# One step of a hybrid DeltaNet and attention block on one core: the opening in groups of 4, 2 and 2, two direct tiles per FFN, and a pinned order at the delta rule

## The chip, the core and the metric

The kernel runs on one core of a Trainium2 chip. TensorE (PE in the rows) multiplies matrices, VectorE (DVE) and ScalarE (ACT) work elementwise, GpSimd (POOL) also, and the queue of SyncE (SP) issues nearly all DMAs. The metric is the device time of one execution in microseconds: the median of three runs was 1587.57 (1587.5 to 1593.31).

## The reference, cut to what matters

One layer works on 128 prompt tokens and 512 latent tokens, 640 in all, of width 1024. Every sublayer begins with an RMS norm whose result is scaled and shifted by vectors that come from a conditioning vector through a large matrix (`ada_w`, nine vectors of 1024 for each of two conditionings).

```python
mod = silu(c) @ ada_w + ada_b             # shift, scale, gate, three times
x = x + 0.5*gate1 * swiglu(modulate(rms_norm(x, norm_ffn1), shift1, scale1), w13, w2)
h = modulate(rms_norm(x, norm_mix), shift2, scale2)
...
x = x + gate2 * merged
x = x + 0.5*gate3 * swiglu(modulate(rms_norm(x, norm_ffn2), shift3, scale3), w13, w2)

def swiglu(h, w13, w2):                   # w13: 1024 x 5632, w2: 2816 x 1024
    a, b = split(h @ w13, 2)
    return (silu(a) * b) @ w2
```

The delta rule is a gated linear attention over chunks, run forwards and backwards for four heads. In each chunk the lower triangular matrix `eye + strict(beta * (k k^T) * decay)` is inverted; the state then passes from chunk to chunk.

## The kernel before, in words

All activations lie transposed: the 1024 channels are eight blocks of 128 partitions, the 640 tokens are two halves of 320 columns. Precision comes from splitting: each operand is a high part (`hh`, `wh`) and a low part (`hl`, `wl`), and each product is three matmuls, high by high, low by high and high by low (`accumulate_step`, line 176). ScalarE makes the high part by a cast, VectorE the low part by a subtraction (`parts`, lines 127 and 131).

**The opening** (lines 1437 to 1460 and `modulation_part`). The inputs are loaded, transposed by TensorE and squared by ScalarE for the norm. The shift and scale vectors of the first FFN are made in four groups of two channel blocks: eight DMAs bring 2 MB of `ada_w`, TensorE multiplies (line 321), VectorE copies the result (line 329), TensorE transposes it (line 332), VectorE adds the bias and forms the scale (lines 337 to 345). Then `modulated` writes the operands of these two blocks: VectorE multiplies (line 403), ScalarE adds the shift and rounds (line 407), VectorE takes the low part (line 409). The first FFN weights are split by ScalarE and GpSimd. The matmuls of the first product are held behind the modulation's by `kpins`.

**An FFN** (`ffn`). The hidden width of 2816 is 22 tiles of 128. The first `DIRECT` tiles take the two products of a tile one after the other over eight blocks. The others (`product_pair`, line 206) take both at once as 2x2 block products by a scheme of seven products over four blocks each; GpSimd prepares four combined weights (lines 570 to 573). The scheme needs combined operands: T1 to T3 (`combined_operands`, lines 529 to 538, behind the second tile) and T4 (`last_operand`, lines 551 to 557, behind the last direct tile). Each tile ends with its low part `gl` (line 495). The tiles go in rounds (`ROUNDS`): after each, `w2` takes the round's tiles to the eight output blocks, and VectorE adds the result to the residual (line 444). The first FFN also carries the other modulation matmuls between its tiles (`between`, line 280). In the last round the last four output blocks go by halves, so that the norm of the next sublayer can begin on one half.

**The delta rule** (`delta`). `delta_front` builds the decay matrices E (subtraction of a column per head at line 986) and the triangular matrix, masked by GpSimd (line 1009); `delta_prep` inverts it in seven levels, each with matmuls, a masking by VectorE that writes P (line 1048), and copies by ScalarE; `delta_step` moves the states, with three products by GpSimd (lines 1090 to 1102). A few remaining z projections run between the first front and the first level; the gate products are spread between the delta rule's matmuls.

**What sets the order.** A planner orders the instructions of each engine when the kernel is built: of those that are ready in its plan, the one earliest in the program goes first. `high_priority(offset=n)` moves instructions n places forward; `issue_after(ins)` puts the instructions of a block behind `ins` on their engine. On the chip every engine works in that fixed order, and an instruction that waits holds all behind it. Tiles with a tag share a number of buffers, and a new tile waits until an old one is released.

## Time and profile before

| | us |
|---|---|
| median of three runs | 1587.57 |
| the profiled execution | 1587.36 |
| its span | 1585.6 |
| TensorE busy | 1541.3 |
| VectorE busy | 1093.8 |
| ScalarE busy | 655.0 |
| GpSimd busy | 290.9 |

The span runs from the first to the last instruction of the profiled execution; busy times are sums over an engine's instructions. A line number in a row is that of the kernel before. An entry such as `wl<-wraw,wh` names what is written and what is read. The time in brackets is how long the engine stood idle before, with what ended that.

### The profile page before, as it was taken

The page shows a single profiled execution, that of the slowest core. Times are in us where ns is not written, and L with a number is a line of the kernel's source. Part 1 is how long each engine was busy: PE and PEld are TensorE (multiplying, and loading weights), DVE is VectorE, ACT ScalarE, POOL GpSimd, SP SyncE. Part 2 cuts the span into 40 slices and gives each one's busy share as a digit, 9 for nine tenths or more (in the row PEclk, how much of TensorE's full clock was granted, in tenths as well). Part 3 has the DMA queues.
Part 4 walks back from the last instruction along what each step waited for, and adds up shares of the span by engine and source line. Part 5 has one row for each costly group of instructions (what it writes and reads, how often), then busy time and mean ns, then how long its engine had stood idle before and what let it go on. Part 6 is the DMA issues. An engine that isn't in the chain of part 4 may idle for free.

```text
span 1585.6 us, 28490 instructions
## 1 busy us (share of the span) xinstructions
PE 1541.3 (97%) x11242; PEld 1460.2 (92%) x11242; DVE 1093.8 (69%) x2317; ACT 655.0 (41%) x1210; POOL 290.9 (18%) x242
## 2 busy tenths in 40 slices
PE   6999999999999899999899999999999999999998
PEld 4889999999998898789889999899899999999997
DVE  6967675757667658886666655775697776767666
ACT  5434242323334545655445544323353433334335
POOL 2022222213120110000221222100005131323210
PEclk9999999999999899999999999999999999999999
DMA  9655444544225341114433324445022323232312
GB/s 328 192 163 174 127 151 147 166 148 133 95 83 148 90 120 48 55 54 130 152 119 99 99 79 122 144 146 160 27 72 76 110 60 111 61 100 67 94 54 67
DMA packets 220784, 181.17 MB, mean 114 GB/s; under 512 B 16160, under 2 KB 198109, under 8 KB 220651
## 3 DMA queue, kind: packets, MB, share of 16 engines
q1 hardware_dynamic: 220395, 179.29, 36.7%
q8 instruction: 89, 1.46, 0.4%
q14 instruction: 44, 0.36, 0.1%
q0 software_dynamic: 256, 0.06, 0.0%
HBM read 161.59 MB, written 16.42 MB: 112 GB/s over the span
## 4 chain that ended last, share of the span: by engine, by line
PE 88%; DVE 7%; DMA 2%; ACT 1%; issue 1%; POOL 0%; SPq 0%; DVEq 0%; POOLq 0%; ACTq 0%
PE big L176 32%; PE aux L206 21%; PE aux L176 12%; PE aux L163 9%; PE big L206 8%; PE aux L280 2%; DVE ht L403 1%; DVE hl L409 1%; PE aux L160 1%; DVE wl L131 1%; DVE cacc L860 1%; DMA wraw<-ffn_w 1%; DMA araw<-ada_w 1%; PE aux L1337 0%; DMA qe<-grows 0%
## 5 line engine op out<-in xcount | busy, mean ns | idle before, releaser
L127 ACT CAST wh<-wraw 128x1024 fp32r<-128x1024 f32 (+1 forms) x147 | 151.8, 1033 | 282.4 <-PE aux L176 99.0
L131 DVE TENSOR_TENSOR wl<-wraw,wh 128x1024 fp32r<-128x1024 f32 (+1 forms) x145 | 180.0, 1242 | 79.8 <-ACT wh L127 78.4
L176 PE MATMUL big<-hh,wh 128*128 128x320 f32 x768 | 191.0, 322 | 7.1 <-ACT hh L407 3.5
L176 PE MATMUL big<-hl,wh 128*128 128x320 f32 x768 | 194.5, 322 | 2.0 <-DVE hl L409 1.4
L176 PE MATMUL big<-hh,wl 128*128 128x320 f32 x768 | 189.0, 317 | 0.4 <-DVE wl L131 0.4
L570 POOL TENSOR_TENSOR ss<-wraw 128x512 f32<-128x512 f32 x38 | 51.0, 1342 | 713.2 <-DMA wraw<-ffn_w 522.5
L127 ACT CAST sh<-ss 128x512 fp32r<-128x512 f32 x152 | 92.6, 621 | 181.0 <-POOL ss L571 85.6
L131 DVE TENSOR_TENSOR sl<-ss,sh 128x512 fp32r<-128x512 f32 x152 | 132.0, 878 | 47.6 <-ACT sh L127 46.7
L206 PE MATMUL aux<-th,sh 128*128 128x320 f32 x456 | 140.9, 309 | 2.0 <-DVE x L444 2.0
L176 PEld LDWEIGHTS big<-hh,wh 128*128 128x128 f32 x768 | 130.3, 192 | 13.4 <-ACT hh L407 6.5
L206 PE MATMUL aux<-tl,sh 128*128 128x320 f32 x456 | 140.9, 309 | 0.0
L206 PE MATMUL aux<-th,sl 128*128 128x320 f32 x456 | 140.7, 309 | 0.0
L176 PEld LDWEIGHTS big<-hl,wh 128*128 128x128 f32 x768 | 132.3, 191 | 7.1 <-DVE hl L409 4.7
L176 PEld LDWEIGHTS big<-hh,wl 128*128 128x128 f32 x768 | 132.3, 191 | 5.3 <-issue 4.2
L176 PE MATMUL big<-gh,wh 128*128 128x320 f32 x352 | 89.0, 313 | 0.0
L444 DVE SCALAR_TENSOR_TENSOR x<-big,gate,x 128x128 f32<-128x128 f32 (+2 forms) x181 | 67.7, 424 | 30.0 <-PE big L176 29.7
L176 PE MATMUL big<-gl,wh 128*128 128x320 f32 x352 | 87.7, 310 | 0.0
L206 PEld LDWEIGHTS aux<-th,sh 128*128 128x128 f32 x456 | 85.6, 188 | 2.3 <-DVE x L444 2.3
L176 PE MATMUL big<-gh,wl 128*128 128x320 f32 x352 | 87.4, 309 | 0.0
L206 PEld LDWEIGHTS aux<-tl,sh 128*128 128x128 f32 x456 | 85.6, 188 | 0.0
L206 PEld LDWEIGHTS aux<-th,sl 128*128 128x128 f32 x456 | 85.6, 188 | 0.0
L1048 DVE TENSOR_TENSOR P<-aux,lv 128x512 f16<-128x512 f32 x70 | 48.2, 689 | 50.1 <-PE aux L163 50.1
(374 smaller groups left out, 3918.6 us busy)
## 6 DMA issues: line engine op xcount, KB each, us to landing
wraw<-ffn_w SPq DMA_DIRECT2D x120, 512.0 KB, 3.9
araw<-ada_w SPq DMA_DIRECT2D x56, 512.0 KB, 5.6
wraw<-w_in SPq DMA_DIRECT2D x35, 512.0 KB, 3.8
araw<-ada_w SPq DMA_DIRECT2D x32, 256.0 KB, 6.5
gd<-stage SPq DMA_DIRECT2D x16, 320.0 KB, 2.8
wraw<-ffn_w SPq DMA_DIRECT2D x12, 384.0 KB, 3.2
wraw<-w_out SPq DMA_DIRECT2D x8, 512.0 KB, 4.3
xd<-x SPq DMA_DIRECT2D x8, 320.0 KB, 2.3
```

Of the source, the lines that this page charges most:

```text
L127: nc.scalar.copy(hi, raw)
L131: nc.vector.tensor_sub(lo, raw, hi.bitcast(F32))
L160: self.marks.append(self.nc.tensor.transpose(*args))
L163: self.marks.append(self.nc.tensor.matmul(*args, **kw))
L176: self.nc.tensor.matmul(ps[h], lhsT=wt[:, k, c0 : c0 + P], rhs=xt[:, h, :], start=(k == 0 and j == 0), stop=(k == len(xs) - 1 and j == 2),)
L206: nc.tensor.matmul(ps, lhsT=wt[:, k * P : (k + 1) * P], rhs=xt, start=(k == 0 and j == 0), stop=(k == n - 1 and j == 2),)
L280: nc.tensor.matmul(ps[32 * g : 32 * g + 32], lhsT=self.s32[:, k, :], rhs=raw[:, g * 256 : (g + 1) * 256], start=(k % 2 == 0), stop=(k % 2 ...
L403: mark = nc.vector.scalar_tensor_tensor(t[:, cols], X[d][:, h, cols], A[:, d, v : v + 1], rb[:, cols], op0=ALU.mult, op1=ALU.mult)
L409: nc.vector.scalar_tensor_tensor(lo[:, cols], t[:, cols], self.mod[:, m_shift, d, v : v + 1], hi[:, cols].bitcast(F32), op0=ALU.add, op1=A ...
L444: nc.vector.scalar_tensor_tensor(X[:, h, cols], ps[:, cols], gate[:, d, v : v + 1], X[:, h, cols], op0=ALU.mult, op1=ALU.add)
L570: nc.gpsimd.tensor_tensor(f[0], b[:, :n], b[:, n:], op=ALU.add)
L1048: nc.vector.tensor_tensor(P16, p1, mask, op=ALU.mult)
```

## The change

- The opening's groups are four, two and two channel blocks instead of four times two. `araw` has one buffer per tile, four of the large and six of the small size. The row factors of the norm come ahead of the first group, and x is multiplied by them ahead of its scale (`scaled`): four blocks before the first group, four pinned behind the first group's scale vector.
- The operands are then written by `modulated_first`: scale and shift by ScalarE for even blocks and by VectorE for odd ones, then a cast by ScalarE and a difference by VectorE.
- The first two weights are split by ScalarE and VectorE, like all others. The first tile's matmuls are written in four steps of two blocks, over both of its products; the second and the third are pinned behind the last matmul of the next modulation group.
- `DIRECT` is 2, the rounds are of 2, 4, 4, 4, 4 and 4 tiles, and the first two tiles call `between` with 3 and 2.
- At the delta rule the subtractions on E of all later chunks are pinned behind the first P of the backward direction, and the GpSimd products of `delta_step` behind the first triangular mask of the backward direction.

```diff
@@ -37,9 +37,9 @@
 OFF_QB, OFF_KB, OFF_VB, OFF_G = 2064, 2576, 2704, 2832
 CB = 648
 LEVELS = [1, 2, 4, 8, 16, 32, 64]
-ROUNDS = [(0, 3), (3, 7), (7, 11), (11, 15), (15, 19), (19, 22)]
+ROUNDS = [(0, 2), (2, 6), (6, 10), (10, 14), (14, 18), (18, 22)]
 KH = KD // 2
-DIRECT = 3
+DIRECT = 2
 
 C_ID = 0
 C_TRI = C_ID + P
...
@@ -123,12 +123,9 @@
             hi, lo = (self.tile(self.phase, [P, n], F32R, tag, self.nsh) for tag in ("sh", "sl"))
         else:
             hi, lo = (self.tile(self.wpool, [P, KD * P], F32R, tag, self.nwh)[:, :n] for tag in ("wh", "wl"))
-        with self.tc.high_priority(offset=0 if self.first_weights else 20):
+        with self.tc.high_priority(offset=20):
             nc.scalar.copy(hi, raw)
-            if self.first_weights:
-                nc.gpsimd.tensor_tensor(lo, raw, hi.bitcast(F32), op=ALU.subtract)
-            else:
-                nc.vector.tensor_sub(lo, raw, hi.bitcast(F32))
+            nc.vector.tensor_sub(lo, raw, hi.bitcast(F32))
         return hi, lo
 
...
@@ -303,46 +300,60 @@
             op=ALU.add,
         )
 
-    def modulation_part(self, m0, g):
+    def modulation_part(self, m0, d0, nd):
 
         nc, a = self.nc, self.a
-        ps = self.aux_tile()
+        n = nd * P
+        ps = self.aux_tile()[:, 0:n]
         for q in range(4):
-            if q % 2 == 0:
-                both = self.tile(self.phase, [P, 2, D], F32, "araw", 6)
-            raw = both[:, q % 2].rearrange("p (k m f) -> p k m f", k=2, m=2)
+            raw = self.tile(self.phase, [P, 2, 2, n], F32, f"araw{nd}", 4 if nd == 4 else 6)
             src = a["ada_w"][0, q * 256 : (q + 1) * 256, m0 * D : (m0 + 2) * D]
-            src = src.rearrange("(k p) (m f) -> p k m f", p=P, m=2)[:, :, :, g * 256 : (g + 1) * 256]
+            src = src.rearrange("(k p) (m f) -> p k m f", p=P, m=2)[:, :, :, d0 * P : d0 * P + n]
             for k in range(2):
                 nc.sync.dma_start(raw[:, k], src[:, k])
             for m in range(2):
                 for k in range(2):
                     j = 2 * m + k
                     last = nc.tensor.matmul(
-                        ps[32 * j : 32 * j + 32, 0:256],
+                        ps[32 * j : 32 * j + 32],
                         lhsT=self.s32[:, 2 * q + k, :],
                         rhs=raw[:, k, m, :],
                         start=(q == 0),
                         stop=(q == 3),
                     )
-        r = self.tile(self.small, [P, 256], F32, "modr", 2)
-        nc.vector.tensor_copy(r, ps[:, 0:256])
-        p2 = self.aux_tile()
-        for h in range(2):
+        r = self.tile(self.phase, [P, n], F32, "modq", 1)
+        nc.vector.tensor_copy(r, ps)
+        p2 = self.aux_tile()[:, 0:n]
+        for h in range(nd):
             nc.tensor.transpose(p2[:, h * P : (h + 1) * P], r[:, h * P : (h + 1) * P], self.ident)
-        pv2 = p2[:, 0:256].rearrange("p (h m k r) -> p m k h r", h=2, m=2, k=2)
+        pv2 = p2.rearrange("p (h m k r) -> p m k h r", h=nd, m=2, k=2)
         for m in range(2):
-            dst = self.mod[:, m0 + m, 2 * g : 2 * g + 2, :]
-            b0 = (m0 + m) * 8 + 2 * g
+            dst = self.mod[:, m0 + m, d0 : d0 + nd, :]
+            b0 = (m0 + m) * 8 + d0
             nc.vector.tensor_tensor(
-                dst, pv2[:, m, 0, :, 0:2], self.vecT[:, b0 : b0 + 2].unsqueeze(2).to_broadcast([P, 2, 2]), op=ALU.add
+                dst, pv2[:, m, 0, :, 0:2], self.vecT[:, b0 : b0 + nd].unsqueeze(2).to_broadcast([P, nd, 2]), op=ALU.add
             )
             nc.vector.tensor_tensor(dst, dst, pv2[:, m, 1, :, 0:2], op=ALU.add)
-        self.kpins.append(last)
+        return last
+
+    def modulated_first(self, hs, xn, A, m_shift, d):
+
+        nc = self.nc
+        for h in range(2):
+            t = self.tile(self.phase, [P, HT], F32, "ht", self.nht)
+            hi, lo = (x[:, h, :] for x in hs[d])
+            for v, cols in PIECES[h]:
+                A1, shift = A[:, d, v : v + 1], self.mod[:, m_shift, d, v : v + 1]
+                if d % 2:
+                    nc.vector.tensor_scalar(t[:, cols], xn[d][:, h, cols], A1, shift, op0=ALU.mult, op1=ALU.add)
+                else:
+                    nc.scalar.activation(t[:, cols], xn[d][:, h, cols], AF.Identity, bias=shift, scale=A1)
+            nc.scalar.copy(hi, t)
+            nc.vector.tensor_sub(lo, t, hi.bitcast(F32))
 
     def scale_columns(self, m, at, t, d0=0, n=KD):
 
-        self.nc.vector.scalar_tensor_tensor(
+        return self.nc.vector.scalar_tensor_tensor(
             t[:, d0 : d0 + n],
             self.mod[:, m, d0 : d0 + n],
...
@@ -425,7 +436,7 @@
                 if h and d == 2:
                     with self.tc.issue_after(mark.ins):
                         list(last)
-        self.by_half = DIRECT
+        self.by_half = 3
         return hs
 
     def add_square(self, acc, x, first):
...
@@ -488,14 +499,13 @@
                     if f == DIRECT - 1:
                         self.last_operand(hs, B)
                 else:
-                    self.kpins = []
                     self.product_pair(w13, f * P, D_FF + f * P, B, s)
                 for h in (1, 0):
                     nc.scalar.copy(gh[:, h], s[:, h])
                     nc.vector.tensor_sub(gl[:, h], s[:, h], gh[:, h].bitcast(F32))
                 gs.append((gh, gl))
                 if between:
-                    between(2 if f < 2 else 1)
+                    between(1 if f > 1 else 3 - f)
 
             two = {}
...
@@ -982,10 +992,11 @@
             row = dr * 20 + c * 4
             E = self.tile(pool, [P, W], F32, "E", 4)
             nc.sync.dma_start(E, self.grows[row : row + 4, :].rearrange("a b -> (a b)").partition_broadcast(P))
-            for h in range(H_A):
-                nc.vector.tensor_scalar(
-                    E[:, hs[h]], E[:, hs[h]], self.ge[:, 0, dr, c, h : h + 1], None, op0=ALU.subtract
-                )
+            with self.behind_opening():
+                for h in range(H_A):
+                    nc.vector.tensor_scalar(
+                        E[:, hs[h]], E[:, hs[h]], self.ge[:, 0, dr, c, h : h + 1], None, op0=ALU.subtract
+                    )
             nc.vector.tensor_scalar(E.bitcast(I32), E.bitcast(I32), 0x7FFFFFFF, None, op0=ALU.bitwise_and)
             nc.scalar.activation(E, E, AF.Exp, scale=-1.0)
...
@@ -1006,10 +1017,11 @@
                     L[:, hs[h]], Es[dr][:, hs[h]], self.nbeta[:, c, 4 * dr + h : 4 * dr + h + 1], gram[:, hs[h]],
                     op0=ALU.mult, op1=ALU.mult,
                 )
-            nc.gpsimd.affine_select(
+            mark = nc.gpsimd.affine_select(
                 out=L, in_=L, pattern=[[0, H_A], [sg, P]], base=0, channel_multiplier=-sg,
                 compare_op=ALU.is_gt, fill=0.0,
             )
+            self.opened[1] = self.opened[1] or (dr and mark)
             M16 = self.tile(pool, [P, H_A, P], F16, "M16", 4)
             nc.vector.tensor_tensor(M16, heads(L), idb, op=ALU.add)
...
@@ -1025,6 +1037,12 @@
             units[c, dr] = [aT]
         self.fronts[c] = (Ls, Ms)
         yield
+
+    def behind_opening(self, pool=0):
+
+
+        mark = self.opened[pool]
+        return self.tc.issue_after(mark.ins) if mark else ExitStack()
 
     def delta_prep(self, pool, scan_pool, c, units):
 
...
@@ -1045,9 +1063,10 @@
                         p1[:, h], lhsT=Ms[dr][:, h], rhs=Um[dr][:, h] if n else self.id16, start=True, stop=True
                     )
                 P16 = self.tile(pool, [P, H_A, P], F16, "P16", 4)
-                nc.vector.tensor_tensor(P16, p1, mask, op=ALU.mult)
+                mark = nc.vector.tensor_tensor(P16, p1, mask, op=ALU.mult)
                 if n == 0:
                     Un = P16
+                    self.opened[0] = self.opened[0] or (dr and mark)
                 else:
                     p3 = heads(self.aux_tile())
                     for h in range(H_A):
...
@@ -1087,21 +1106,24 @@
         heads = lambda t: t.rearrange("p (h f) -> p h f", h=H_A)
         X = self.tile(pool, [P, W], F32, "X", 2)
         nc.sync.dma_start(heads(X), self.vd[c])
-        nc.gpsimd.tensor_tensor(
-            heads(X), heads(X), self.beta[:, c, 4 * dr : 4 * dr + 4].unsqueeze(2).to_broadcast([P, H_A, P]),
-            op=ALU.mult,
-        )
+        with self.behind_opening(1):
+            nc.gpsimd.tensor_tensor(
+                heads(X), heads(X), self.beta[:, c, 4 * dr : 4 * dr + 4].unsqueeze(2).to_broadcast([P, H_A, P]),
+                op=ALU.mult,
...
@@ -1206,6 +1228,7 @@
                 if not first:
                     yield [self.delta_output(pool, c)]
 
+        self.opened = [None, None]
         start = front(0)
         next(start, None)
         next(start, None)
...
@@ -1259,9 +1282,6 @@
 
     def after(self, k):
 
-
-        if self.kpins:
-            return self.tc.issue_after(self.kpins[min(3, k // 2 + 1)].ins)
         if self.nfill == 0:
             return ExitStack()
...
@@ -1329,7 +1349,7 @@
             src = a["x_prompt"][0] if t == 0 else a["x_sample"][0, (t - 1) * P : t * P, :]
             xt = self.tile(self.phase, [P, D], F32, "xin", NCH)
             nc.sync.dma_start(xt, src)
-            jk = self.tile(self.phase, [P, D], F32, "xsq", 2)
+            jk = self.tile(self.phase, [P, D], F32, "xsq", 1)
             nc.scalar.activation(jk, xt, AF.Square, accum_out=ss[:, t : t + 1])
             for d0 in (0, 4):
                 ps = self.aux_tile()
...
@@ -1442,22 +1461,52 @@
                     self.phase = ada
                     A1 = self.tile(self.const, [P, KD, 2], F32, "A1")
                     hs = self.operand_tiles(KD)
-                    for g in range(4):
-                        self.modulation_part(0, g)
-                        self.scale_columns(1, 72, A1, 2 * g, 2)
-                        if g == 0:
-                            rb = []
-                            for cuts in (((0, 0, P), (1, 0, P), (2, 0, HD)), ((2, HD, HD), (3, 0, P), (4, 0, P))):
-                                o, columns = 0, []
-                                for t, t0, n in cuts:
-                                    columns.append((r[:, t : t + 1], t0, n, o))
-                                    o += n
-                                rb.append(self.half_rows(columns))
-                            self.first_weights = True
-                            first = [self.wcols(a["ffn1_w13"][0], c) for c in (0, D_FF)]
-                            self.first_weights = False
+                    rb = []
+                    for cuts in (((0, 0, P), (1, 0, P), (2, 0, HD)), ((2, HD, HD), (3, 0, P), (4, 0, P))):
+                        o, columns = 0, []
+                        for t, t0, n in cuts:
+                            columns.append((r[:, t : t + 1], t0, n, o))
+                            o += n
+                        rb.append(self.half_rows(columns))
+                    xp = inner.enter_context(pool("xn", side="right"))
+                    xn = [self.tile(xp, [P, 2, HT], F32, "xn", KD) for _ in range(KD)]
+
+                    def scaled(d):
                         for h in range(2):
-                            self.modulated(hs, X, rb[h], A1, 0, h, (2 * g, 2 * g + 1))
+                            nc.vector.tensor_tensor(xn[d][:, h], X[d][:, h], rb[h], op=ALU.mult)
+
+                    def first_steps(d0, after=None):
+                        with self.tc.issue_after(after.ins) if after else ExitStack():
+                            for ps, w in zip(first, ws):
+                                for d in (d0, d0 + 1):
+                                    self.accumulate_step(ps, w, hs, d, 0, (0, 1))
+
+                    for d in range(4):
+                        scaled(d)
+                    self.modulation_part(0, 0, 4)
+                    mark = self.scale_columns(1, 72, A1, 0, 4)
+                    pa = self.tile(self.big, [P, 2, 512], F32, "big", 2)
+                    first = [[pa[:, h, 0:HT] for h in range(2)], [self.aux_tile()[:, 0:HT] for _ in range(2)]]
+                    ws = []
+                    for d in range(4):
+                        if d < 2:
+                            ws.append(self.wcols(a["ffn1_w13"][0], (0, D_FF)[d]))
+                        self.modulated_first(hs, xn, A1, 0, d)
+                    first_steps(0)
+                    with self.tc.issue_after(mark.ins):
+                        for d in range(4, KD):
+                            scaled(d)
+                    last = self.modulation_part(0, 4, 2)
+                    self.scale_columns(1, 72, A1, 4, 2)
+                    first_steps(2, last)
+                    for d in (4, 5):
+                        self.modulated_first(hs, xn, A1, 0, d)
+                    last = self.modulation_part(0, 6, 2)
+                    self.scale_columns(1, 72, A1, 6, 2)
+                    first_steps(4, last)
+                    for d in (6, 7):
+                        self.modulated_first(hs, xn, A1, 0, d)
+                    first_steps(6)
                 with pool("g1", side="right") as self.phase:
                     gates = {m: self.tile(self.const, [P, KD, 2], F32, f"gate{m}") for m in (2, 5, 8)}
 

```

## Rows read from the trace of the kernel before

**Rows 1.** The page, part 1: busy time, share of the span and instructions of each engine.
```profile
PE 1541.3 (97%) x11242; PEld 1460.2 (92%) x11242; DVE 1093.8 (69%) x2317; ACT 655.0 (41%) x1210; POOL 290.9 (18%) x242
```

**Rows 2.** Stretches of 20 us: busy us (instructions) by engine, clock, DMA share, GB/s.
```profile
500.00:520.00 20.00, 17.13 (x97) 16.04 (x95) 14.82 (x43) 6.51 (x14) 0.00 (x0) 0.83 0.48 149
...
760.00:780.00 20.00, 14.07 (x91) 13.41 (x90) 14.63 (x23) 6.24 (x10) 9.33 (x9) 0.83 0.53 163
...
1160.00:1180.00 20.00, 20.00 (x138) 20.00 (x138) 20.00 (x46) 8.91 (x20) 0.00 (x0) 1.00 0.19 60
```

**Rows 3.** What TensorE waited for: us in total, times, longest.
```profile
PE aux L163 <- DVE P L1048: 5.9, 1, 5.9
...
PE aux L206 <- DVE x L444: 2.0, 1, 2.0
```

**Rows 4.** DMA view, 0 to 45 us: GB/s in 40 slices of 1.125 us.
```profile
GB/s 0 55 134 377 387 393 404 390 361 361 347 350 346 349 316 290 291 311 349 349 348 348 352 338 353 345 351 347 351 354 336 351 348 386 411 366 313 293 300 289
```

**Rows 5.** Timeline of the opening: start us, us, engine line op out<-in xcount [idle before].
```profile
12.45 0.69 DVE L1341 COPY x<-aux 128x512 f32<-128x512 f32 x1 [0.18 <-PE aux L1337]
...
16.45 1.93 PE L321 MATMUL aux<-araw,s 128*32 128x256 f32 x32 [3.20 <-issue]
...
18.92 0.44 PE L332 MATMUL aux<-ident,modr 128*128 128x128 f32 x2 [0.54 <-DVE modr L329]
...
20.05 0.16 DVE L345 SCALAR_TENSOR_TENSOR A<-mod,vecT 128x4 f32<-128x4 f32 x1
...
47.78 1.01 DVE L409 SCALAR_TENSOR_TENSOR hl<-ht,mod,hh 128x320 fp32r<-128x320 f32 x2
...
51.84 0.46 PE L176 MATMUL aux<-hh,wl 128*128 128x320 f32 x2
```

**Rows 6.** Groups by line and shape: busy us, mean ns of one | idle before.
```profile
L131 DVE TENSOR_TENSOR wl<-wraw,wh 128x1024 fp32r<-128x1024 f32 x133 | 168.6, 1268 | 76.0 <-ACT wh L127 74.6 <-PE aux L163 0.9
...
L570 POOL TENSOR_TENSOR ss<-wraw 128x512 f32<-128x512 f32 x38 | 51.0, 1342 | 713.2 <-DMA wraw<-ffn_w 522.5 <-DVE gl L495 85.9 <-DVE sl L131 40.6
```

**Rows 7.** Timeline of VectorE in the second FFN, tiles 1 and 2.
```profile
1151.51 1.29 DVE L529 TENSOR_TENSOR ht<-hh,hl 128x320 f32<-128x320 f32 x3
...
1167.33 1.29 DVE L529 TENSOR_TENSOR ht<-hh,hl 128x320 f32<-128x320 f32 x3
1168.54 1.29 DVE L534 TENSOR_TENSOR ht<-ht,ht 128x320 f32<-128x320 f32 x3
...
1170.15 0.48 DVE L495 TENSOR_TENSOR gl<-s,gh 128x320 fp32r<-128x320 f32 x1
...
1172.89 0.48 DVE L551 TENSOR_TENSOR ht<-hh,hl 128x320 f32<-128x320 f32 x1
...
1180.79 0.49 DVE L557 TENSOR_TENSOR hl<-ht,hh 128x320 fp32r<-128x320 f32 x1
```

**Rows 8.** Timeline of TensorE: one modulation step; the end of tile 1, second FFN.
```profile
69.32 1.07 PE L280 MATMUL aux<-araw,s 128*32 128x256 f32 x16
...
1165.10 0.46 PE L176 MATMUL aux<-hh,wl 128*128 128x320 f32 x2
```

**Rows 9.** Timeline of the start of the delta rule, all engines.
```profile
755.02 1.28 DVE L986 TENSOR_SCALAR E<-E,ge 128x128 f32<-128x128 f32 x5 [1.31 <-DMA E<-grows]
...
762.88 0.64 POOL L1009 TENSOR_SCALAR_AFFINE_SELECT L<-L 128x512 f32<-128x512 f32 x1
...
767.18 3.51 DVE L986 TENSOR_SCALAR E<-E,ge 128x128 f32<-128x128 f32 x5
...
773.00 0.68 DVE L1048 TENSOR_TENSOR P<-aux,lv 128x512 f16<-128x512 f32 x1
...
773.74 0.61 PE L163 MATMUL aux<-id,P 128*128 128x128 f16 x4 [5.93 <-DVE P L1048]
...
775.21 0.73 PE L176 MATMUL big<-hl,wh 128*128 128x320 f32 x2
```

**Rows 10.** A stretch of 2 us behind that wait, columns as in rows 2.
```profile
776.00:778.00 2.00, 2.00 (x9) 1.80 (x9) 0.15 (x1) 0.00 (x0) 0.00 (x0) 0.50 0.90 184
```

18 lines of the change are left out of this document (10 added, 8 removed).

## The prediction

> **What bounds the kernel now.** The first view is the busy line: TensorE is busy 97% of the span [rows 1]. So only two things can shorten the kernel much: fewer matmuls, or fewer of the stretches in which TensorE waits. The table of twenty-microsecond stretches shows where those are [rows 2]: the reader is to see a clock of 0.83 and only 97 and 91 matmuls at 500:520 and 760:780, where a full stretch holds 138. The list of waits gives two owners: one of 5.9 us at the delta rule (TensorE for P of VectorE) and one of 2.0 us for the residual of the first FFN [rows 3]. The opening is a third such place. The last row of rows 2 is as important: at 1160:1180, with TensorE full, VectorE is busy 20.00 of 20 us. There the second engine has nothing left to give. A full stretch also gives the price of a matmul of 320 columns: 20/137 = 0.146 us.
>
> **Fewer matmuls.** A direct tile is 2 products x 8 blocks x 3 x 2 halves = 96 matmuls; a tile by seven products is 7 x 4 x 3 = 84. One tile per FFN changes sides, so 24 matmuls go: 24 x 0.146 = **-3.5 us**. The rounds still cover 22 tiles; the number of other matmuls, weight loads and residual additions is the same.
>
> **The opening.** Before, the scale vector of the first group is written at 20.2 us, the last half operand at 48.7, and the first tile's last matmul starts at about 52 [rows 5]. After, the first group is four tiles wide, so its 4.19 MB must land first. The slices of 1.125 us [rows 4] add up to the inputs' 2.69 MB at 9.8 us; at the 390 GB/s of the slices with long rows the group lands 10.7 us later, at about 21.0 with the landing (at the 350 GB/s of the later slices: 22.3). The Trainium skill, "SBUF — State Buffer", section "A bandwidth-pool intuition that's wrong", gives a core about 358 GB/s from HBM; by that, as an estimate, the group would come 1.0 us later than at 390; the slices of 377 to 404 in this trace lie above it. Then the last eight matmul records of double width (1.93/32 x 2 x 8 = 1.0), the copy of 512 columns (0.7), four transposes (2 x 0.44 = 0.9), and five short VectorE steps of 0.2 (1.0): the scale vector is there at 24.6 us, 4.4 us later than now.
>
> From there I count VectorE, in pitches: three additions of 320 columns start 1.21 us after one another [rows 7], so 0.40 each. Even blocks: two differences, 0.8. Odd blocks: those and three scalings; not in the trace in this form, bounded by 0.26 (128 columns, first of rows 9) and 0.40, so 0.9 for three. Four and four: 4 x 0.8 + 4 x 1.7 = 10.0. Eight scalings by the row factor that stand behind the first group: 3.2 (the other eight lie before 24.6, under the transfer, at no cost). The low halves of the first two weights, which leave GpSimd, and the first of the next tile: 3 x 1.2 = 3.5 by [rows 6]. Modulation steps of groups two and three: 2 x 1.35. Sum 19.4, so 44.0, and 45 with half a microsecond of waiting for each later group. ScalarE has 24 steps of 320 columns and 3 of 1024 in the same time, some 15 us at VectorE's durations, and is covered. The row factors move ahead of the first group and the squares share one scratch buffer on the engine that writes them in order: no cost, since the first group's transfer covers both. The transfers are covered too: 1.05 MB of weights at 300 GB/s and 4.19 MB at 350 end at 36. The last 12 matmuls follow (1.8): first tile done at 46.7 instead of 52.2, **-5.5 us**. If the waits between groups are 2 us each it is -2.5; if the scalings run in gaps it is -7.
>
> **Two direct tiles and the VectorE queue.** This is the term that speaks against the change. The sums for the seven products (L529 to L538: 36 VectorE operations, 14.5 us) and those for T4 (L551 to L557: 16 operations, 6.4 us) now both stand behind tile 1 and ahead, in program order, of the low half gl of tile 1, for which the round's matmuls wait. In the second FFN the sums start at 1151.5 and tile 1 is done at 1165.4 [rows 7, 8]. In the trace they end about 1171, and T4's operations run from 1172.9 to 1181.2 while TensorE is under tile 2. That cover is gone. After: the sums end about 1170 (without tile 2's first low weight, 1.2, in between), T4's 6.4 us later, and with the round's first low weight (0.6 at 512 columns) gl comes about 1177. TensorE can do about 32 of the 96 matmuls of the round without them (4.7 us), to 1170.1, and idles 7 us. After an idle stretch TensorE's clock falls: behind the 5.9 us at the delta rule it was 0.50, half speed, and 9 matmuls stood in 2 us instead of 13.7 [rows 10]; a pair took 0.73 us, a pair at full speed 0.46 [rows 9, 8]. The mean of 0.83 over 760:780 is 6.8 us at half speed, some 5 of them at work; they cost 1.7 (at 9 for 13.7) to 2.5 us, and I take 2.1. Together **+9.1 us**. The lower end is 0: in the trace gl ran early, at 1170.15, in a gap of the sums [rows 7]. The upper end is in the rivals. I take the upper of the near values, since the T4 additions are ready then and fill such gaps first.
>
> In the first FFN the tile 1 matmuls end at 46.7 + 14.1 + 3 x 1.07 (the modulation's matmuls, [rows 8]) = 64.0. VectorE from 45: 3.2 for s and gl of both tiles, 1.2, three modulation copies (1.1), 14.5, 6.4, 0.6: 72. TensorE has 4.7 and two more modulation steps (2.5) to do: 71.2. So 1 to 3 idle us, with some clock: **+3 us** (0 to 8). The 2.0 us of [rows 3] I leave as it is; it is the same queue one tile later.
>
> **The end of the first FFN.** The last round has four tiles instead of three, so the final half of its last four columns is 48 matmuls and not 36. They run under the norm of the other half, whose VectorE chain sets the end (17.13 busy us at a clock of 0.83 [rows 2]): 12 x 0.146 = **-1.8 us** (0 to -4, if the clock stays up). At the second FFN nothing follows that they could cover: 0.
>
> **The delta rule.** In the trace five of the subtractions on E for the next chunk start at 767.2 and take 3.51 us beside GpSimd's products, against 1.28 alone [rows 9]; P, for which TensorE waits, runs at 773.0, the matmuls start at 773.74 after 5.9 us, and then at half clock. The pin puts those subtractions behind the P of the other direction, and the GpSimd products behind the second triangular mask, which ran at 762.9 behind two of them. P can then run when its matmuls are done (about 767): -5.9 for the idle time, -2.1 for the clock as above, and +0.7 for the round trip of the first P (0.68 in rows 9), which has no other cover: **-7.3 us** (-4 to -9). What is late next: nothing soon, since the next chunk's E is wanted only after the seven levels of this one. The pins in later chunks are passed long before, at no cost. The DMA queue issues the same transfers in the same order there.
>
> **Sum.** -3.5 - 5.5 + 9.1 + 3 - 1.8 - 7.3 = -6.0. The profiled execution took 1587.36 (span 1585.6 and 1.8 around it); the median is 1587.57, the same. Forecast 1581.4 us.
>
> **The rivals.**
> Holes (0.28): gl and the first weight find gaps in the sums, as at 1170.15. Then the second FFN costs 1 and the first 0: -6.0 - 8.1 - 3 = -17.1, 1570. Against it: VectorE at 20.00 of 20.
> GpSimd in the queue (0.12): the four subtractions that prepare the first seven-product weights (1.3 us each [rows 6]) fall into the very stretch in which VectorE works off the sums, now that the round before is shorter. The five E subtractions above took 2.7 times their time beside GpSimd. At that ratio 5.3 us of GpSimd work costs VectorE 3.3 us for each of two weight sets; with the second round trip at half clock some 8 us in each FFN more: -6 + 16 = +10, 1597. It decides against the change from 6 us on. For it: rows 9; against it: nss buffers let only one set run ahead. The Trainium skill, "SBUF — State Buffer", section "SBUF: two separate sides", calls the port pair of the two engines an exclusive lock, held for a whole instruction; the stretched subtractions agree, and by the rule the loss per set would be the full 5.3 us, 2 more.
> The pins do little (0.15): after them another operation (a weight's low half, 1.2 us) holds P, or E is late for the next chunk. Only 2 are left of the 7.3: -0.7, 1587. Against it: of what stands ahead of P in rows 9, most is what is moved.
> Forecast as summed: 0.45.
>
> **How the numbers follow.** 0.5% (7.9 us) is about what a measurement of this kernel can tell from no change. Faster by more (below 1579.6): holes nearly whole, 0.26, and 0.10 of the forecast's case, whose own range is 1574 to 1589: 0.36. Slower by more (above 1595.5): most of the GpSimd case, 0.09. The rest, 0.55, is no change. The range leaves out half of each outer case: 1569 to 1596.
>
> **What would show it.** The first tile's last matmul near 47 us; 192 matmul records fewer at line 176 and 168 more at line 206; TensorE without a wait for P over 1 us and a clock of 1.0 at the delta rule; a TensorE gap of several us behind tile 1 of the second FFN, released by gl or its weight, with VectorE in L551 to L557. The forecast is wrong if that gap is under 2 us (then faster), or if VectorE's own operations are stretched there (then slower).

## The result, and the profile after

The changed kernel takes 1604.29 us (median of five runs, 1603.49 to 1605.35) against 1587.57: a ratio of 1.0107 (95% interval 1.0091 to 1.0124), 17.0 us slower. The forecast was 1581.4, its range 1569 to 1596. Below, ratios are also given in us, as parts of 1587.6. A line of the old kernel has another number in the new one: L176 is L173, L206 is L203, L131 is L128, L163 is L160, L444 is L455, L495 is L505, L551 to L557 are L561 to L567, L570 to L573 are L580 to L583, L1048 is L1066.

Part 1 of the page after, against [rows 1]:
```profile
PE 1540.2 (96%) x11186; PEld 1457.2 (91%) x11186; DVE 1109.3 (69%) x2329; ACT 661.5 (41%) x1222; POOL 308.4 (19%) x248
```
TensorE works 1.1 us less in a span that is 16.1 us longer. The stretches of 20 us after, with the columns of [rows 2], show where; two stretches of before stand in the second block:
```profile
60.00:80.00 20.00, 14.32 (x112) 12.31 (x104) 18.32 (x47) 7.80 (x19) 0.00 (x0) 0.92 0.36 118
80.00:100.00 20.00, 18.08 (x124) 15.64 (x124) 14.62 (x33) 4.26 (x7) 6.42 (x4) 0.83 0.63 198
500.00:520.00 20.00, 19.93 (x138) 19.70 (x137) 14.19 (x32) 7.55 (x14) 0.00 (x0) 1.00 0.43 119
760.00:780.00 20.00, 20.00 (x148) 19.79 (x148) 14.09 (x29) 8.75 (x12) 9.66 (x9) 1.00 0.80 251
...
1160.00:1180.00 20.00, 13.65 (x87) 12.98 (x85) 20.00 (x51) 9.72 (x23) 0.00 (x0) 0.89 0.07 24
1180.00:1200.00 20.00, 18.82 (x113) 18.82 (x114) 18.73 (x40) 6.31 (x10) 7.24 (x5) 0.85 0.41 114
1220.00:1240.00 20.00, 16.75 (x111) 16.05 (x110) 17.07 (x25) 9.11 (x16) 5.59 (x4) 1.00 0.27 84
```
```profile
60.00:80.00 20.00, 19.83 (x155) 17.62 (x148) 17.97 (x40) 6.60 (x14) 0.00 (x0) 1.00 0.58 192
...
1220.00:1240.00 20.00, 20.00 (x138) 19.95 (x138) 15.58 (x24) 9.19 (x15) 5.63 (x4) 1.00 0.40 120
```
The delta rule (760:780) is now full, at a clock of 1.00; the wait for P that is left stands 10 us later, at 782. The two FFNs, full before, have holes: one behind the direct tiles, and a second one 40 us later, in the first pairs. The list of TensorE's waits after (us in total, times, longest), against [rows 3]:
```profile
PE big L173 <- DVE wl L128: 11.7, 3, 7.5
...
PE aux L391 <- DVE rr L223: 4.5, 1, 4.5
PE big L173 <- DVE gl L505: 3.8, 1, 3.8
...
PE aux L203 <- ACT gh L504: 1.9, 1, 1.9
PE aux L203 <- DVE u L612: 1.9, 1, 1.9
...
PE aux L160 <- DVE P L1066: 1.4, 1, 1.4
```
P costs 1.4 us where it cost 5.9. The weights and gl behind tile 1 cost 15.1 us in the two FFNs together (7.5 for a weight in the first, 3.7 and 3.8 in the second; the other 0.4 us of the first row lie elsewhere), and the opening waits 4.5 us for the row factors.

I add up per stage what TensorE loses: its idle time, plus, in steps of 2 us, its busy time times what the granted clock lacks to 1. From before to after: opening and first two tiles 12.6 to 20.8; first FFN to 200 us 2.2 to 17.2; end of the first FFN 6.5 to 1.7; start of the delta rule, with the wait for P, 8.8 to 1.6; second FFN to 1250 us 0 to 13.9. The first pair of numbers needs care: in this one trace of before the clock stayed up in the opening, and in two of three others it did not (last section). The differences add up to 25.1 us; the span grew by 16.1, of which the 24 matmuls that went take back 3.5, and the other 5.5 I can't assign.

### The profile page after: what moved, and what is told of

It is laid out like the page before. It is cut to its first block, busy times and chain, and to the rows that moved or that the text cites. A ratio compares the mean times of both kernels' runs of the same rounds, so it can differ in the third digit from the quotient of the medians.

```text
span 1601.7 us, 28416 instructions
## 1 busy us (share of the span) xinstructions
PE 1540.2 (96%) x11186; PEld 1457.2 (91%) x11186; DVE 1109.3 (69%) x2329; ACT 661.5 (41%) x1222; POOL 308.4 (19%) x248
## 4 chain that ended last, share of the span: by engine, by line
PE 81%; DVE 9%; DMA 3%; ACT 3%; issue 2%; POOL 2%; DVEq 0%; POOLq 0%; SPq 0%; ACTq 0%
PE big L173 32%; PE aux L203 18%; PE aux L173 10%; PE aux L160 9%; PE big L203 7%; DMA wraw<-ffn_w 2%; PE aux L277 1%; DVE wl L128 1%; ACT wh L127 1%; PE aux L157 1%; DVE sl L128 1%; PE aux L317 1%; DVE cacc L870 1%; POOL ss L581 1%; DVE tl L548 1%
## 5 line engine op out<-in xcount | busy, mean ns | idle before, releaser
L128 DVE TENSOR_TENSOR wl<-wraw,wh 128x1024 fp32r<-128x1024 f32 (+1 forms) x145 | 181.9, 1256 | 78.5 <-ACT wh L127 75.4
L580 POOL TENSOR_TENSOR ss<-wraw 128x512 f32<-128x512 f32 x40 | 57.7, 1442 | 727.9 <-DMA wraw<-ffn_w 436.4
L173 PE MATMUL big<-hh,wh 128*128 128x320 f32 x736 | 185.1, 322 | 9.9 <-ACT hh L351 3.4
L173 PE MATMUL big<-hl,wh 128*128 128x320 f32 x736 | 185.1, 322 | 1.0 <-DVE hl L420 0.5
L173 PE MATMUL big<-hh,wl 128*128 128x320 f32 x736 | 180.7, 318 | 0.5 <-DVE wl L128 0.4
L128 DVE TENSOR_TENSOR sl<-ss,sh 128x512 fp32r<-128x512 f32 x160 | 139.5, 882 | 39.4 <-ACT sh L127 38.8
L203 PE MATMUL aux<-th,sh 128*128 128x320 f32 x480 | 149.7, 312 | 7.0 <-ACT gh L504 1.9
L203 PE MATMUL aux<-tl,sh 128*128 128x320 f32 x480 | 149.3, 311 | 0.0
L203 PE MATMUL aux<-th,sl 128*128 128x320 f32 x480 | 149.0, 310 | 0.0
L173 PEld LDWEIGHTS big<-hh,wh 128*128 128x128 f32 x736 | 125.1, 191 | 16.4 <-ACT hh L351 5.8
L173 PEld LDWEIGHTS big<-hl,wh 128*128 128x128 f32 x736 | 125.8, 191 | 7.3 <-DVE hl L420 4.0
L173 PEld LDWEIGHTS big<-hh,wl 128*128 128x128 f32 x736 | 126.1, 191 | 3.7 <-issue 2.6
L173 PE MATMUL big<-gh,wl 128*128 128x320 f32 x352 | 89.0, 314 | 11.3 <-DVE wl L128 11.3
L203 PEld LDWEIGHTS aux<-th,sh 128*128 128x128 f32 x480 | 90.8, 189 | 8.5 <-issue 2.7
L455 DVE SCALAR_TENSOR_TENSOR x<-big,gate,x 128x128 f32<-128x128 f32 (+2 forms) x181 | 67.7, 423 | 40.1 <-PE big L173 39.7
L173 PE MATMUL big<-gl,wh 128*128 128x320 f32 x352 | 89.1, 314 | 3.8 <-DVE gl L505 3.8
L203 PEld LDWEIGHTS aux<-tl,sh 128*128 128x128 f32 x480 | 90.8, 189 | 0.0
L203 PEld LDWEIGHTS aux<-th,sl 128*128 128x128 f32 x480 | 90.8, 189 | 0.0
L173 PE MATMUL big<-gh,wh 128*128 128x320 f32 x352 | 90.0, 317 | 0.1
L1066 DVE TENSOR_TENSOR P<-aux,lv 128x512 f16<-128x512 f32 x70 | 48.2, 689 | 48.2 <-PE aux L160 48.2
```

Source lines behind the costliest of these rows:

```text
L128: nc.vector.tensor_sub(lo, raw, hi.bitcast(F32))
L173: self.nc.tensor.matmul(ps[h], lhsT=wt[:, k, c0 : c0 + P], rhs=xt[:, h, :], start=(k == 0 and j == 0), stop=(k == len(xs) - 1 and j == 2),)
L203: nc.tensor.matmul(ps, lhsT=wt[:, k * P : (k + 1) * P], rhs=xt, start=(k == 0 and j == 0), stop=(k == n - 1 and j == 2),)
L455: nc.vector.scalar_tensor_tensor(X[:, h, cols], ps[:, cols], gate[:, d, v : v + 1], X[:, h, cols], op0=ALU.mult, op1=ALU.add)
L580: nc.gpsimd.tensor_tensor(f[0], b[:, :n], b[:, n:], op=ALU.add)
L1066: mark = nc.vector.tensor_tensor(P16, p1, mask, op=ALU.mult)
```

## The experiments

The kernel before ran beside each. "against before" is the ratio, its 95% interval and the us that the ratio makes. In a filled opening, matmuls whose result nobody reads stand where TensorE is idle. e6 leaves out the sums for T4, and e14 the four weight sums of GpSimd.

| run | what it is | median us | against before |
|---|---|---|---|
| e1 | the change without its FFN part | 1581.72 | 0.9965 [0.9949, 0.9980] -5.6 |
| e2 | before, and the pins | 1581.18 | 0.9964 [0.9948, 0.9980] -5.7 |
| e3 | the change, T4 right behind gl | 1603.41 | 1.0093 [1.0076, 1.0111] +14.8 |
| e4 | the change, row factors behind the first group | 1603.09 | 1.0097 [1.0081, 1.0114] +15.4 |
| e5 | the change, T4 in the first pair | 1593.80 | 1.0051 [1.0037, 1.0064] +8.1 |
| e6 | the change, no T4 sums | 1590.33 | 1.0019 [1.0008, 1.0030] +3.0 |
| e7 | the change, T4 on GpSimd | 1602.71 | 1.0102 [1.0089, 1.0116] +16.2 |
| e8 | e2, round of three put fourth | 1579.89 | 0.9959 [0.9946, 0.9972] -6.5 |
| e9 | the change, three direct tiles | 1592.60 | 1.0038 [1.0025, 1.0052] +6.0 |
| e10 | the change, old rounds | 1609.25 | 1.0138 [1.0122, 1.0154] +21.9 |
| e11 | e8, new opening as in e4, steps later | 1583.83 | 0.9974 [0.9961, 0.9987] -4.1 |
| e12 | e8, T4 in the first pair | 1580.02 | 0.9943 [0.9926, 0.9961] -9.0 |
| e13 | e1, filled opening | 1576.95 | 0.9918 [0.9900, 0.9936] -13.0 |
| e14 | e5, no GpSimd sums | 1584.24 | 0.9971 [0.9955, 0.9987] -4.6 |
| e15 | e13, round of three put fourth | 1573.67 | 0.9912 [0.9896, 0.9928] -14.0 |
| e16 | e8, filled old opening | 1579.37 | 0.9946 [0.9929, 0.9962] -8.6 |

### Which part loses: e1 and e2

```diff
 # e1
-ROUNDS = [(0, 2), (2, 6), (6, 10), (10, 14), (14, 18), (18, 22)]
+ROUNDS = [(0, 3), (3, 7), (7, 11), (11, 15), (15, 19), (19, 22)]
-DIRECT = 2
+DIRECT = 3
...
-                    between(1 if f > 1 else 3 - f)
+                    between(2 if f < 2 else 1)
```


> The change without its FFN part: three direct tiles, the old rounds, the old calls of the modulation; opening and pins stay. Theory A (the loss is in the FFN part: waits of 7.5 us and 7.5 us for the weights and gl behind tile 1, the half clock behind them, and the waits in the first two pairs, about +29 us in both FFNs, against -3.5 for 24 fewer matmuls and -4.8 at the end of the first FFN, so about +20 net): 1584 us, within 3. Theory B (the loss comes from the opening, which ends 2 us later and hands a full VectorE queue on to the first FFN): the first FFN stalls as before this edit, and the time stays above 1592.

> The kernel before with the pins at the delta rule alone. Theory A (the pins take away the 5.9 us wait and the 2.8 us of half clock behind it, and give back 2.5 us at 1000 to 1020, where the trace of after idles more): 1581.4. Theory B (the loss at 1000 to 1020 does not come from the pins): 1579. Theory C (the wait is given back whole in the next chunks): 1587.5, no change. Together with the run without the FFN part this prices the opening: by its end of tile 1 it costs 1.9 us, so that run should be about 2 us slower than this one.

Theory A of the first run holds, and A of the second by its time. The FFN part costs 17.0 + 5.6 = 22.6 us, the pins bring 5.7, and the opening, in which e1 and e2 differ, is +0.1, within some 3.5 us. By trace, the start of the delta rule loses 1.4 us in e2 and not 8.8. Whether the pins give 2.5 us back near 1000 us stays open: from 990 to 1030 TensorE loses 2.9 us before, 4.4 after and 4.1 in e2, but only 1.8 in e1, which has the pins too.

### Place or amount: e3, e5, e6, e7

VectorE and TensorE of the changed kernel behind tile 1 of the second FFN (start, us, engine, line):
```profile
1173.20 0.49 DVE L561 TENSOR_TENSOR ht<-hh,hl 128x320 f32<-128x320 f32 x1
...
1180.64 0.90 DVE L505 TENSOR_TENSOR gl<-s,gh 128x320 fp32r<-128x320 f32 x2
```
```profile
1175.55 0.50 PE L173 MATMUL big<-gh,wl 128*128 128x320 f32 x1 [3.73 <-DVE wl L128]
...
1181.18 0.63 PE L173 MATMUL big<-gl,wh 128*128 128x320 f32 x1 [3.80 <-DVE gl L505]
```
T4 runs from 1173.2 to 1181.9, with two low halves of the other sums, one low half of a weight and gl between its operations, and TensorE waits twice, 7.5 us: the mechanism of the forecast. GpSimd has no part in it; its first operation in this FFN comes later:
```profile
1188.47 1.30 POOL L580 TENSOR_TENSOR ss<-wraw 128x512 f32<-128x512 f32 x1 [184.82 <-DMA wraw<-ffn_w]
```

```diff
 # e3: last_operand behind the loop that writes gl
...
 # e5, in product_pair (and the call behind tile 1 goes)
+        if "T4" not in B:
+            self.last_operand(hs, B)
         p4 = bank()
```


> The changed kernel with the sums for T4 written behind the low half gl of tile 1 instead of ahead of it; all work stays. Theory A (order: gl and the first weight stand behind 6.4 us of T4 on VectorE, and that alone makes TensorE wait and lose its clock): the waits of 7.5 and 7.5 us in the two FFNs fall to about 1.5 each, the clock holds, and the time is about 1588 to 1591. Theory B (amount: VectorE has these 6.4 us to do before the first pair anyway, with the weights and the residual additions behind them): the waits move to the later weights of the round and to the first pair, and the time stays at 1599 to 1605.

> The changed kernel with the sums for T4 written in the first pair, just ahead of the one product that reads them; all work stays. Theory B (amount: from the end of tile 1 to the end of the first pair VectorE has more to do than the 14 us of output products and the 12 us of a pair cover, wherever T4 stands): the waits move once more, into the first pair, and the time stays at 1597 to 1604. Theory A (place: the earlier run moved T4 only behind the first weight, and TensorE then waited for the second one behind it; ahead of its reader T4 holds nobody): the 7.5 us in each FFN go with their clock, and the time is 1586 to 1591.

> The changed kernel without the sums for T4: the product that should read T4 reads the plain operand, so 16 VectorE operations (6.4 us) and 4 of ScalarE per FFN are left out. Theory B (amount): the waits shrink by about 6.4 us and the clock loss behind them with it, in both FFNs: 1604 - 2 x 8 = 1588, and little waiting is left in the first pairs. Theory A (place): the same 1586 to 1591; the two part only if this is much faster than the run with T4 in the first pair. If the loss were the GpSimd products beside VectorE and not T4: 1600 or more.

In e3 gl is early, and TensorE waits for the round's weights behind T4 instead:
```profile
1174.19 0.64 PE L173 MATMUL big<-gh,wl 128*128 128x320 f32 x1 [4.54 <-DVE wl L128]
...
1180.48 0.84 PE L173 MATMUL big<-gh,wl 128*128 128x320 f32 x2 [2.05 <-DVE wl L128]
```
That looked like theory B. In e5, where T4 stands ahead of its reader, 8.9 us go, and in e6, without it, 14.0. Neither theory is whole: place is worth 9, and T4's own time in the first pair 5 more. What stays, 8.6 us between e6 and e1, is not T4 (and e6 has 24 matmuls fewer than e1, 3.5 us, so its stalls cost some 12).

> The changed kernel with the 16 sums and differences for T4 on GpSimd, which is idle there, in the same place of the program. If VectorE's own work is what counts and the two engines work beside each other freely: the time of the run without T4, 1588. If GpSimd's operations hold VectorE up as they stretch its five subtractions of E from 1.28 to 3.51 us at the delta rule: VectorE's queue gets no shorter, and the time is 1598 to 1604.

Moving the 16 operations to the idle engine brings 0.8 us, within the intervals. GpSimd, VectorE and TensorE of that run:
```profile
1167.68 5.21 POOL L561 TENSOR_TENSOR ht<-hh,hl 128x320 f32<-128x320 f32 x1 [168.10 <-DVE ht L544]
1172.86 0.87 POOL L561 TENSOR_TENSOR ht<-th,tl 128x320 f32<-128x320 f32 x1
```
```profile
1172.08 1.13 DVE L455 SCALAR_TENSOR_TENSOR x<-big,gate,x 128x320 f32<-128x320 f32 x3
```
```profile
74.92 2.21 DVE L505 TENSOR_TENSOR gl<-s,gh 128x320 fp32r<-128x320 f32 x2
```
```profile
1182.48 0.90 PE L173 MATMUL big<-gh,wh 128*128 128x320 f32 x2 [3.99 <-ACT wh L127]
```
In the second FFN an addition of 0.87 us took 5.21 beside VectorE, and in the first FFN two of VectorE's differences took 2.21 and not 0.90. The rest of the wait moved to ScalarE: its roundings of T4 now wait for GpSimd's sums, each of which takes 0.87 us where VectorE's take 0.49, and the casts of the weights stand behind them. So the time is as expected, but VectorE's queue did get shorter in the second FFN. The Trainium skill, "Perfetto Trace Analysis", section "Optimizing Scalar/DVE Operations", says that offloading between these two engines might not help; this run agrees, with 0.8 us.

### Cover: e9, e10, e14

> The changed kernel with three direct tiles; the new rounds, opening, pins and calls of the modulation stay. So the first output round of two tiles comes with T4 behind tile 2 and not behind tile 1. Theory A (the missing direct tile costs: T4 and the making of the first pairs' weights lose the 14 us of TensorE work that covered them): both stalls go, 24 matmuls come back (3.5 us), and the time is 1579 to 1583. Theory B (the short first output of 14 us costs, since VectorE's residual additions, low halves and T1 to T3 do not fit under it): the stalls stay, 1592 or more.

> The changed kernel with the old rounds of 3, 4, 4, 4, 4 and 3 tiles and two direct tiles, so that the first pair stands ahead of the first output and right behind tile 1. Theory A (the missing direct tile costs, wherever the output stands): the first pair now waits for T1 to T3, its own weights and T4 with nothing under it, 6 to 9 us in each FFN with the clock, and the time is 1590 to 1600. Theory B (the short first output costs): the output is 21 us again, the stalls go, and the time is 1578 to 1583.

Neither edit is harmless alone: the new rounds with three direct tiles cost 6.0 + 5.6 = 11.6 us over e1, two direct tiles in the old rounds 27.5, both together 22.6. The longest wait of e10 is that for the low halves of the first pair's weights, with nothing under it:
```profile
PE big L203 <- DVE sl L128: 12.6, 1, 12.6
```
So A holds in e10, with more than it expected, and B in e9, just: a first output of 14 us does not cover what VectorE has to do either. In e9's trace, of its fastest run, TensorE waits 1.5 and 1.6 us in the first outputs of the two FFNs, and 3.2 and 4.9 us ahead of the first pairs behind them. The two parts do not add up to 22.6, so how much of it belongs to either edit can't be told.

```diff
 # e14: e5, and the halves of the raw weights in place of the four sums on GpSimd
-        f = [self.tile(self.phase, [P, n], F32, "ss", self.nss) for _ in range(4)]
...
-            nc.gpsimd.tensor_tensor(f[3], a[:, n:], f[1], op=ALU.subtract)
+        f = [b[:, :n], a[:, :n], b[:, :n], a[:, n:]]
```


> The changed kernel with T4 in the first pair, and without the four weight sums of GpSimd in any pair: the halves of the raw weights go in their place, so no operation of GpSimd runs in the FFNs. It tells what the 12 us are that remain between 1593.8 and the 1581.7 of the version without the FFN part. Theory G (GpSimd's sums beside VectorE stretch its operations, 0.48 to 1.58 us for one of 320 columns, in the first pairs): the waits in the first pairs go, 1583 to 1587. Theory L (the first pairs' weights come late because their transfers, casts and low halves begin behind the round's own, with or without GpSimd): 1590 to 1594.

12.7 us go against e5, and by trace they go in the first pairs: from 100 to 150 us TensorE loses 8.8 us in e5 and nothing in e14, from 1185 to 1260 5.8 and 1.6. That is theory G by time. The last products of a pair on VectorE between 1150 and 1245 us (count, busy, mean ns), in the changed kernel and in e14:
```profile
L613 DVE TENSOR_TENSOR s<-s,u 128x320 f32<-128x320 f32 x3 | 2.5, 849 | 0.0
```
```profile
L608 DVE TENSOR_TENSOR s<-s,u 128x320 f32<-128x320 f32 x4 | 1.9, 484 | 0.0
```
and two of them beside GpSimd in the changed kernel:
```profile
1209.57 1.55 DVE L611 TENSOR_TENSOR s<-s,u 128x320 f32<-128x320 f32 x1 [0.27 <-ACT s L608]
...
1212.75 1.58 DVE L613 TENSOR_TENSOR s<-s,u 128x320 f32<-128x320 f32 x1
```
```profile
1209.47 1.30 POOL L580 TENSOR_TENSOR ss<-wraw 128x512 f32<-128x512 f32 x1 [3.78 <-DVE sl L128]
...
1212.24 1.74 POOL L582 TENSOR_TENSOR ss<-wraw,wraw 128x512 f32<-128x512 f32 x1
```
In e5 the product of line 613 takes 756 ns in the mean and that of line 611 480. The kernel before has stretched rows too (849 ns), and TensorE loses nothing there from 1150 to 1250 us; that tile 2 and a longer first output cover them is my reading, which no run shows by itself. e14 takes away two things at once, the stretching of VectorE and GpSimd's own 6 us per pair between transfer and cast; how the 12.7 us divide between them stays open.

### The opening: e4, e11, e13, e16

TensorE and VectorE of the changed kernel in the opening:
```profile
17.39 2.90 PE L391 MATMUL aux<-ident,rr 128*128 128x128 f32 x12 [4.54 <-DVE rr L223]
20.21 4.51 PE L317 MATMUL aux<-araw,s 128*32 128x512 f32 x32
...
29.46 0.64 PE L173 MATMUL big<-hh,wh 128*128 128x320 f32 x1 [3.19 <-ACT hh L351]
...
54.00 0.46 PE L173 MATMUL aux<-hh,wl 128*128 128x320 f32 x2
```
```profile
26.98 0.17 DVE L356 SCALAR_TENSOR_TENSOR A<-mod,vecT 128x8 f32<-128x8 f32 x1
```
All 32 matmuls of the first group run behind the row factors, from 20.2 us on, and so for the most part behind the transfer, whose end the last of them wait for until 21.4 in e4. The scale vector is written at 27.0 and the first tile ends at 54.5.

> The changed kernel with the row factors of the norm written behind the first modulation group instead of ahead of it. Theory A (the row factors' transposes wait for VectorE until 17.4 us, run at half clock until 20.2, and hold the 32 matmuls of the first group behind them, so that all of these run after their data has landed instead of beside it): the first scale vector comes 3 us earlier than at 27.0, and the kernel is 2 to 3.5 us faster than the changed one, about 1601. Theory B (TensorE is full from 29.5 us on and sets the end of the first tile; the rows that now come later hold the first operands): within 1 us of the changed kernel, 1604.

The scale vector came at 24.6, as forecast, but the first operand only 1.0 us earlier (28.43), behind the row factors that now came later and the halves of the first weights. Theory B holds.

> A kernel with the new opening, the pins, three direct tiles and the round of three put fourth (3, 4, 4, 3, 4, 4); in the opening the row factors are written behind the first group, and the first tile's steps are pinned behind the transposes of the next group and no longer behind its last matmul. In the run with the row factors alone the second group's transposes stood 2.3 us, and the third group's matmuls 4 us, behind these steps on TensorE. Theory A (TensorE's order keeps the scale vectors back): the first tile ends 3 us earlier and the time is 1576 to 1577.5, against 1579.9 with the old opening. Theory B (TensorE is full there and the clock of the first 34 us decides): 1579 to 1581, the same as with the old opening.

There is no gain, but a loss of 2.4 us against e8: tile 1 now waited 3.75 us for its first weight, and the third group stood behind that wait. So this run does not settle whether TensorE's order keeps the scale vectors back: VectorE waited 0.5 us for the second group's transposes, and 2.3 in the changed kernel. I went on to the clock.

```diff
 # e13, ahead of the row factors; four more behind the first group
+                    warm = self.aux_tile()
+                    for _ in range(5):
+                        nc.tensor.matmul(warm, lhsT=self.ident, rhs=xall[:, 0:2, 0, 0 : HT - 64], start=True, stop=True)
```


> The new opening, the pins and three direct tiles in the old rounds, with nine matmuls of 512 columns whose result nobody reads added on TensorE: five ahead of the row factors and four behind the transposes of the first group. Theory A (TensorE's idle 4.5 us ahead of the row factors and 3.2 us ahead of the first operands let its clock fall to half, 4.6 to 6 us of lost pace in every trace of the new opening, and that is what the opening's gain went into): the granted clock stays at 1.0 to 40 us, the first tile ends 2 to 4 us earlier, and the time is 1578 to 1579.5, against 1581.7 without them. Theory B (the chain over VectorE and ScalarE sets the first tile's end, and TensorE would wait where it now runs slowly): the clock stays up and the time stays at 1581 to 1583.

The same stretch in e1 and in e13:
```profile
28.00:36.00 8.00, 6.84 (x29) 4.13 (x32) 8.00 (x21) 5.71 (x13) 0.00 (x0) 0.57 0.72 230
```
```profile
28.00:36.00 8.00, 7.51 (x60) 4.79 (x60) 7.88 (x21) 4.26 (x11) 0.00 (x0) 1.00 1.06 330
```
The clock stands at 1.00 and 60 matmuls are done instead of 29. The modulation step behind tile 1 starts at 65.8 instead of 69.4, and the kernel gains 4.8 us by medians (7.4 by ratios). Theory A holds.

> The version with the filled new opening (1576.95), with the round of three put fourth as in the run with the last round of four. If the two gains add (1.3 us for the round, by medians; 3 by the idle time at the end of the first FFN): 1573.5 to 1576. If the end of the first FFN gains nothing once the opening is shorter: 1577.

> The old opening with the pins and the round of three put fourth (1579.9), and four matmuls that nobody reads added ahead of the first modulation group, where TensorE idles 3.2 us; the twin of the filled new opening. Theory A (the old opening's clock fell in one trace of three only, so there is little to give back, and the new opening is worth 3 to 4 us once its clock holds): 1578 to 1580. Theory B (filling is the whole gain and the new opening is worth nothing): as the filled new opening, 1574 to 1576.

e15 and e16 differ in the opening alone: the new one is worth 5.4 us by ratios (within some 3.6), 5.7 by medians, of which 2.7 show at the modulation step behind tile 1 (65.99 against 68.69). The two traces differ in later stretches as well, by about 2 us each at 66:200, 480:560 and 760:800; what the opening has to do with those is not shown. Filling the old opening brought nothing that can be told (0.5 us by medians, 2.1 by ratios), as theory A has it. e15 is the fastest version here, 0.9912 of the kernel before; its gain on e13 (3.3 us by medians, 1.0 by ratios) can't be told from none.

### The round of three, and T4 with three direct tiles: e8 and e12

> The kernel before with the pins, and with the round of three tiles put fourth instead of last (3, 4, 4, 3, 4, 4), so that the last round has four tiles as in the change, while three tiles stay direct and the first round is the old one. Theory A (the idle time and the half clock at the end of the first FFN, 6.5 us in the trace of before and 1.7 in that of after, shrink because the last half product is longer): 3 to 5 us faster than the pins alone, 1577. Theory B (that gain came with something else): 1581, as the pins alone.

> The kernel before with the pins, the round of three put fourth, and the sums for T4 written in the first pair instead of behind the last direct tile. Theory A (the 2.0 us wait of rows 3 for the residual in the first FFN is the end of VectorE's queue of sums, which T4 lengthens by 6.4 us also with three direct tiles): that wait and the clock behind it go, 2 to 4 us faster than without this edit, 1576 to 1578. Theory B (with three direct tiles T4 is covered by tile 2, and moving it brings the collision with GpSimd in the first pair instead): 1580 to 1583.

By time neither can be told from the run that it was made from: e8 is -0.8 us against e2, e12 -2.5 against e8. By trace, e8 loses 1.7 us at 500:526 where e2 loses 5.1. In e12 the 2.0 us wait of [rows 3] for the residual stayed: it is not T4's queue, as I had assumed.

## Why the prediction was wrong, step by step

- **Fewer matmuls, -3.5.** Right: 192 records fewer at line 176, 168 more at line 206.
- **The opening, -5.5, measured +0.1.** The step that failed is the one that counts VectorE from 24.6 us, gives each later group half a microsecond of waiting, and lets TensorE follow. Two things were missing in it. One is the clock: the first operand came at 29.5, TensorE had stood idle for 4.5 and 3.2 us before, and it did its next matmuls at half clock (0.57 over 28:36). I had priced that effect at the delta rule [rows 10] and left it out here; with it the row factors are not without cost either, and the scale vector is written at 27.0 and not at 24.6. The other is the waiting of VectorE for the later groups, whose transposes stand behind the first tile's matmuls on TensorE. In the changed kernel, and with 2.28 in e13:
```profile
42.34 0.16 DVE L333 TENSOR_TENSOR mod<-aux,vecT 128x4 f32<-128x4 f32 x1 [2.30 <-PE aux L328]
```
In e13, with the clock at 1.00, the scale vector is written at 24.9, as forecast. But VectorE then waits 4.6 us in all until the last operand where the sum has 1.0, and the first tile ends at 50.3 and not at 46.7:
```profile
49.83 0.46 PE L173 MATMUL aux<-hh,wl 128*128 128x320 f32 x2
```
So the 5.4 us between e15 and e16 lie near the forecast partly by luck: the trace shows 2.7 of them in the opening, close to the -2.5 that the prediction gives for waits of 2 us at each group.
- **The second FFN, +9.1.** The gap came where described, and near its size: 3.73 + 3.80 us, and 3.1 of clock. Not in this term are 3.3 us in the first pairs.
- **The first FFN, +3 (0 to 8), measured +15.0.** The failed step: "TensorE can do about 32 of the 96 matmuls" and two modulation steps first. Each block's matmuls stand in the order high, low, weight's low half; TensorE did one modulation step and 6 matmuls, and then waited 7.5 us for that weight:
```profile
73.92 0.46 PE L173 MATMUL big<-gl,wh 128*128 128x320 f32 x2
81.92 0.64 PE L173 MATMUL big<-gh,wl 128*128 128x320 f32 x1 [7.54 <-DVE wl L128]
```
In the second FFN, where the sum has the same 32, it did 14 before its first wait and 6 more before the second. Behind the wait of the first FFN come 2.5 us of clock, and 5 in the first pairs.
- **The end of the first FFN, -1.8.** The trace shows -4.8 there, most of it clock that no longer falls; by time e8 can't tell it.
- **The delta rule, -7.3, measured -5.7 (-8.3 to -3.2).** Right, with a wait for P of 1.4 us, a little over the 1 us that was named as the sign.
- **The rivals.** I gave GpSimd in the queue 0.12, as a case beside the forecast. It did not come where that rival has it: while VectorE works off the sums and T4, GpSimd does nothing (its first operations start at 93.1 and 1188.5 us, T4 ends at 82.3 and 1181.9), and T4's operations keep their 0.48 to 0.49 us. What came is a loss in the first pairs behind that, on top of the forecast's case: 12.7 us go with GpSimd's sums (forecast 16; how much of it is stretching stays open), 8.9 with T4's place (forecast 12.1). The forecast's -6.0 with that rival's +16 and without the opening's -5.5 would have been 1603; that this is near the measured time is luck, since neither the places nor the single terms are those of the sum. The Trainium skill, "SBUF — State Buffer", section "SBUF: two separate sides", says of the two engines' shared ports that whoever starts first keeps them for the whole instruction. e7 agrees that the two hold each other up, but its addition of 0.87 us took 5.21, over some ten operations of VectorE and not one.

## What to carry to other kernels

A TensorE stage that is cut shorter takes its cover away from everything the second engine does under it: add up that engine's work from the last operand to the next stage's first use, with its stretched operations, against the matmuls that can run without its results in the order in which they stand, and not only at the one instruction that seems late. Where a change opens an idle stretch on TensorE, price the half clock behind it too; a few matmuls nobody reads can be cheaper than the idle time. Losses that can come together belong in one sum.

## What the hardware showed unexpectedly

The fall of the clock in the opening is not fixed: of four traces with the old opening and its 3.2 us of idle time, it fell in two (4.8 and 6.1 us lost) and stayed in two; in all eleven traces with the new one unfilled it fell (2.8 to 6.2); in all three filled ones it stayed at 1.00. And in e7 one operation of GpSimd took six times its time beside a full VectorE queue, where I had only seen VectorE stretched. It ended 0.8 us after VectorE turned from differences of SBUF tiles to residual additions, which take one operand from PSUM, where the matmuls' results lie; beside those, GpSimd's next sums took 0.87 us each and three residual additions 1.13, as they do in the changed kernel without GpSimd (1.13 to 1.14).
